# One hybrid decoder layer step with product-key experts: layout of the streamed one-hots, early expert products, gather pacing, buffers of the closing norms

## The chip, the cores and the metric

The kernel runs on one core of one Trainium2 chip, as one program on that core. The metric is device time in microseconds (us). TensorE (PE in the profile), its weight loads (PEld), VectorE (DVE), ScalarE (ACT), GpSimd (POOL) and SyncE (SP) each run a stream of instructions of their own; SP here does nothing but start DMA transfers.

## What is computed

One layer for 512 prompt tokens and 8 sample tokens (one new token each), width 1024, all in f32: a norm, one input projection into attention and retention heads, the two mixers, an output projection with residual; then a layer of single-neuron experts, and a final norm. The change lies in the expert layer and the final norm:

```
def _peer_block(xb, w_pq, sub_keys, peer_u, peer_v):
    q = (xb @ w_pq).reshape(blk, PEER_HEADS, 2, PEER_HALF)            # 8 heads, two halves of 128
    s = jnp.einsum('thcd,hcnd->thcn', q, sub_keys).astype(jnp.float32)  # 128 keys a half
    sv, si = lax.top_k(s, PEER_TOPK)                                  # 16 of 128, each half
    cand = (sv[:, :, 0, :, None] + sv[:, :, 1, None, :]).reshape(blk, PEER_HEADS, PEER_TOPK * PEER_TOPK)
    cidx = (si[:, :, 0, :, None] * PEER_N_KEYS + si[:, :, 1, None, :]).reshape(...)
    best, pos = lax.top_k(cand, PEER_TOPK)                            # 16 of the 256 pairs
    eid = jnp.take_along_axis(cidx, pos, -1)                          # expert i * 128 + j
    g = jax.nn.softmax(best, -1).astype(xb.dtype)
    u = peer_u[eid]
    a = jax.nn.gelu(jnp.einsum('thkd,td->thk', u, xb))
    return jnp.einsum('thk,thkd->td', g * a, peer_v[eid])
...
    h = hp + _mixer_output(attn_o, ret_o, rg, ret_gn_g[l], w_out[l])
    hp = _channel(h, norm2_g[l], w_pq[l], ...)                        # h + _peer(_rmsnorm(h))
y_prompt = _rmsnorm(hp, norm_f_g)
```

Each token thus uses 8 x 16 = 128 of 16,384 experts; peer_u and peer_v hold 1024 numbers for each expert.

## The kernel before

**Two ways to the same experts.** Prompt tokens 0 to 255 (lists 0 and 1) and the 8 samples (list S) are *gathered*; prompt tokens 256 to 511 (lists 2 and 3) are *dense*.

- A gather step handles one (head, k) of one list: GpSimd starts an indirect DMA that fetches for each of 128 tokens its expert's row (L898) into one of GBUFS = 8 buffers of the pool's tag "rows", and VectorE folds it in, either as a dot with the token (L914, peer_u, into a; its sum is read out by a second short instruction) or as a weighted sum into y (L928, peer_v). Lists 0 and 1 have 256 steps each, list S has 32 steps of 64 partitions (8 samples x 8 heads): 544 in all, each list's after the one before it.
- In the dense way every value of i (the first half of an expert's number) is a product row. `dense_a` multiplies the 128 experts i * 128 + j with the 256 tokens (L869: 8 products of 256 columns, weights ut, loaded by SP at L866 out of a table turned for it) and takes gelu of it (L873, tile ge). `dense_w` multiplies ge by the weight of each pair (L1048, tile big; zero for experts that a token didn't choose). `dense_y` sums over j (L1055: 4 products of 512 columns, against vt, loaded by SP at L1042) into four PSUM banks that stay open over all 128 rows.
- The weights in big come from one-hots: for a group of 8 tokens VectorE compares lists with a ramp (oj, L1026: 128 values of j x 8 tokens; oi, L1027: 64 values of i x 8 tokens), multiplies oi by the weight split into three bf16 parts (oi3, L1029), and TensorE multiplies, for each of the 8 tokens and the 3 parts, oj (as loaded weights) with oi3 (as the stream of 64 columns) (L1034): 24 products a group. ScalarE puts the result into big (L1036). There are 32 groups, once for i below 64 (`scatter(0, n)`, ahead of the first product row's `dense_w`) and once for i from 64 on (`scatter(1, n)`, between the first 64 rows).

**Stages.** Mixers and output projection to about 386 us. Then the product keys: for 8 heads, first of the gathered tokens and samples, then of the dense ones (`product_keys`, L148 projects with w_pq, which SP loads at L127; L805 and L810 give the scores, L814 copies them out, VectorE makes the top-16 lists). Among the dense tokens' heads `between(h)` emits the first EARLY = 96 gather steps; among the 32 groups of `scatter(0, n)` the next SOON = 48, and the first AHEAD = 20 of `dense_a`. The main loop then runs over i: `dense_a(i + 20)`, `dense_y(i - 1)`, `dense_w(i)`, and gather steps at (RATE - EARLY - SOON) / 128 = 3.28 a row. What is left of the steps follows, with the norm of each list (`finish`) at its end, and at the very end the norm of the dense tokens.

**What sets the order.** The source emits instructions in the order above; a scheduler then places them at build time, by a timeline of its own, on each engine, so that a step can stand later in an engine's stream than it is emitted. `tc.issue_after` keeps steps behind a given instruction, `in_order` (L1059) keeps TensorE's products of the main loop as written. SP's queue is followed in order. A tag's buffers go round: UTB = 4 for ut, VTB = 4 for vt, OHB = 2 for the one-hots, AHEAD + 2 for ge.

Of the kernel before, what the change touches and what calls it, by code (L numbers as in the profile page):

```python
# [19 lines left out]
D = 1024  # L20
# [11 lines left out]
GT = 256  # L32
NC = [(0, 256), (256, 520)]
DT = 512 - GT
GBUFS, UTB, VTB, OHB, AHEAD = 8, 4, 4, 2, 20
ORDER = "aayyyy"
FIRST = 6
SCB = 4
# [3 lines left out]
CHUNKS = [0, 64, 128]  # L42
ROWS = max(b - a for a, b in zip(CHUNKS, CHUNKS[1:]))
NG = DT // 8
EARLY, SOON, RATE = 96, 48, 564


@with_exitstack
def step_kernel(ctx, tc, x_prompt, x_sample, cache_k, cache_v, state_ret, norm1_g, w_in, ret_gn_g,
# [38 lines left out]
    def row_bcast(dst, src, n):  # L88
        nc.sync.dma_start(dst, bass.AP(tensor=src.tensor, offset=src.offset, ap=[[0, dst.shape[0]], [1, n]]))
# [786 lines left out]
    def run(g, n=1):  # L876
        for _ in range(n):
            if g is not None:
                next(g, None)
# [19 lines left out]
                                     in_offset=bass.IndirectOffsetOnAxis(ap=d["eid"][:p, h, k:k + 1], axis=0))  # L899
        return t  # L900

    def experts(d, rows):
        p, H = d["p"], d["H"]
        y = pe.tile([128, D], F32, name="y", tag="y")[:p]
        hn = pe.tile([128, D], F32, name="hq", tag="hq")[:p]
        for n, src in enumerate(rows):
            nc.sync.dma_start(hn[n * p // len(rows):(n + 1) * p // len(rows)], src)

        def dots(h):
            a = pe.tile([128, TOPK], F32, name="a", tag="a", bufs=3)[:p]  # L910
            for k in range(TOPK):
                yield
                u = gather(u_tab, d, h, k, "u")
                nc.vector.tensor_tensor_reduce(out=u[:p], in0=u[:p], in1=hn, scale=1.0, scalar=0.0,  # L914
                                               op0=OP.mult, op1=OP.add, accum_out=a[:, k:k + 1])
            w = pe.tile([128, TOPK], F32, name="gw", tag="gw", bufs=3)[:p]
            nc.scalar.activation(w, a, AF.Gelu_apprx_tanh)
            nc.vector.tensor_tensor(out=w, in0=w, in1=d["g"][:p, h, :], op=OP.mult)
            return w

        def sums(h, w):
            for k in range(TOPK):
# [12 lines left out]
        return y

    def finish(halves, p, rows, dst):
# [15 lines left out]
    yp2 = y_p.rearrange("a t d -> (a t) d")  # L953

    def gathered():
        y = yield from experts(lists[0], [hnr[:128, :]])
        finish((y[:, 0:512], y[:, 512:]), 128, slice(0, 128), yp2[0:128, :])
        y = yield from experts(lists[1], [hnr[128:GT, :]])
        finish((y[:, 0:512], y[:, 512:]), 128, slice(128, GT), yp2[128:GT, :])
        y64 = yield from experts(listS, [hnr[GT:, :]] * 8)  # L960
# [5 lines left out]
        finish((yS[:, 0:512], yS[:, 512:]), 8, slice(512, 520), y_s.rearrange("b t d -> (b t) d"))  # L966

    work = gathered()

    def between(h):  # L970
# [46 lines left out]
    def scatter(c, n):  # L1017

        t0 = n * 8
        r0, r1 = CHUNKS[c:c + 2]  # L1020
        ni = r1 - r0
        oj = dw.tile([128, 128, 8], BF16, name="oj", tag="oj", bufs=OHB)
# [13 lines left out]
        nc.scalar.activation(place(c, n), pg_.rearrange("p (t i) -> p t i", i=ni), AF.Copy)  # L1036

# [43 lines left out]
    def ahead():
        for i in range(AHEAD):
            g = dense_a(i)
            for _ in range(2):
                run(g)
                yield
# [88 lines left out]
```

## Time and profile before

| | |
|---|---|
| median of 3 runs | 1840.87 us (1839.99 to 1841.41) |
| the profiled execution | 1843.8 us, span of its records 1842.0 us |
| mean granted TensorE clock | 0.901 of full speed |
| busy: TensorE, VectorE, ScalarE, GpSimd | 1598.4, 1210.3, 366.4, 777.3 us |
| moved by DMA | 488.55 MB, mean 265 GB/s |

The span runs from the first to the last record of the profiled execution. Busy shares over the whole span mix stages with different limits, so the rows further down are by stage. An f32 product leaves two records on TensorE (1888 records of L869 in one bank and 160 in another are 128 rows x 8 products x 2). DMA share is the mean busy share of the core's 16 DMA engines.

### The profile page before, as it was taken

To read this page: it belongs to the slowest core of one execution; us is meant where nothing else is said; L and a number is where in the kernel's file an instruction comes from. 1 tells how busy PE (TensorE), PEld (TensorE's weight loads), DVE (VectorE), ACT (ScalarE), POOL (GpSimd) and SP (SyncE) were. 2 spreads that over 40 slices of the span, in tenths; PEclk is the share of its full clock that TensorE was granted. 3 is DMA by queue.
4 is the path that set the end of the run, shared out by engine and by line. 5 is a ranking of instruction groups with operands and counts; after the bars stand their busy time and mean duration, and the time that the engine had idled before them with its cause. 6 is when DMAs were issued, how large, how long until landed. Compare 5 with 4: busy or idle time off the path is not lost. (4 is left out here: it accounts for less than half of the span.)

```text
span 1842.0 us, 22181 instructions
## 1 busy us (share of the span) xinstructions
PE 1598.4 (87%) x7848; PEld 1206.4 (65%) x7848; DVE 1210.3 (66%) x2835; ACT 366.4 (20%) x727; POOL 777.3 (42%) x672
## 2 busy tenths in 40 slices
PE   5999998989877844789999999999999999999700
PEld 5888875968766734786777777776766666664300
DVE  5556654228999889999656555645555555557687
ACT  5554332532212111231101111111100000000001
POOL 2015521010472785645444332444445545546553
PEclk9999899989988975559999999999999999999955
DMA  5226554343797978668998888888889999999986
GB/s 180 68 70 184 168 164 128 109 155 121 242 367 237 327 270 322 216 189 304 357 331 292 324 311 284 315 322 313 286 298 390 362 361 360 361 348 380 387 255 151
DMA packets 182031, 488.55 MB, mean 265 GB/s; under 512 B 15848, under 2 KB 71704, under 8 KB 181920
## 3 DMA queue, kind: packets, MB, share of 16 engines
q0 software_dynamic: 82208, 295.80, 45.7%
q1 hardware_dynamic: 99712, 191.33, 29.6%
q8 instruction: 62, 1.02, 0.2%
q14 instruction: 49, 0.40, 0.1%
HBM read 477.21 MB, written 9.86 MB: 264 GB/s over the span
## 5 line engine op out<-in xcount | busy, mean ns | idle before, releaser
L898 POOL DMA_INDIRECT u<-in_peer_u,eidL x256 | 328.9, 1285 | 382.2 <-DVE y L928 119.8
L869 PE MATMUL pa<-hnD,ut 128*128 128x256 f32 x1888 | 451.7, 395 | 27.6 <-ACT ge L873 20.8
L1055 PE MATMUL y<-vt,ge 128*128 128x512 f32 x1024 | 460.2, 596 | 9.0 <-DMA vt<-in_peer_v 9.0
L898 POOL DMA_INDIRECT v<-in_peer_v,eidL x256 | 323.3, 1263 | 321.9 <-DVE y L928 148.2
L869 PEld LDWEIGHTS pa<-hnD,ut 128*128 128x128 f32 x1888 | 373.9, 200 | 114.8 <-issue 41.2
L928 DVE SCALAR_TENSOR_TENSOR y<-v,gw,y 128x1024 f32<-128x1024 f32 (+1 forms) x269 | 344.1, 1279 | 30.4 <-DMA v<-in_peer_v,eidL 25.0
L914 DVE CUSTOM_DVE_ANT_0 u<-u,hq 128x1024 f32<-128x1024 f32 (+1 forms) x272 | 324.5, 1221 | 20.9 <-DMA u<-in_peer_u,eidL 20.6
L1055 PEld LDWEIGHTS y<-vt,ge 128*128 128x128 f32 x1024 | 195.8, 191 | 211.4 <-issue 195.3
L1034 PEld LDWEIGHTS <-oj 128*128 128x128 bf16 x1536 | 186.6, 146 | 50.2 <-DVE oi L1029 32.2
L1048 DVE TENSOR_TENSOR ge<-ge,big 128x256 f32<-128x256 f32 x128 | 51.2, 422 | 194.5 <-ACT ge L873 181.3
L1034 PE MATMUL pg<-oi,oj 128*128 128x64 bf16 x1152 | 147.3, 301 | 19.3 <-DVE oi L1029 19.2
L873 ACT ACTIVATE ge<-pa 128x256 f32<-128x256 f32 x118 | 45.3, 384 | 555.9 <-PE pa L869 548.7
L1026 DVE TENSOR_TENSOR oj<-iota,lJ 128x1024 bf16<-128x1024 bf16 x64 | 44.1, 688 | 148.7 <-PE pg L1034 146.2
L117 PE MATMUL pa<-xT,wh 128*128 128x256 f32 (+1 forms) x448 | 135.6, 305 | 3.4 <-ACT xT L113 3.2
L118 PE MATMUL pa<-xT,wh 128*128 128x256 f32 (+1 forms) x448 | 132.5, 296 | 0.1
L119 PE MATMUL pa<-xT,wl 128*128 128x256 f32 (+1 forms) x448 | 130.6, 292 | 0.0
L1036 ACT ACTIVATE big<-pg 128x512 f32<-128x512 f32 x48 | 53.3, 1110 | 221.5 <-PE pg L1034 219.2
L117 PEld LDWEIGHTS pa<-xT,wh 128*128 128x128 f32 x448 | 85.5, 192 | 14.2 <-issue 8.1
L118 PEld LDWEIGHTS pa<-xT,wh 128*128 128x128 f32 x448 | 85.9, 192 | 6.2 <-issue 4.9
L119 PEld LDWEIGHTS pa<-xT,wl 128*128 128x128 f32 x448 | 85.9, 192 | 5.0 <-issue 4.1
L111 DVE TENSOR_TENSOR wl<-raw,wh 128x1024 fp32r<-128x1024 f32 x36 | 44.3, 1232 | 59.8 <-ACT wh L110 59.7
L148 PE MATMUL pa<-hnD,raw 128*128 128x256 f32 x256 | 62.5, 401 | 13.7 <-DMA raw<-in_w_pq 13.7
(464 smaller groups left out, 1725.8 us busy)
## 6 DMA issues: line engine op xcount, KB each, us to landing
ut<-in_u_turned SPq DMA_DIRECT2D x128, 512.0 KB
vt<-in_peer_v SPq DMA_DIRECT2D x128, 512.0 KB
raw<-in_w_pq SPq DMA_DIRECT2D x16, 1024.0 KB
raw<-in_w_in SPq DMA_DIRECT2D x28, 512.0 KB
kv<-in_cache_k_win POOLq DMA_DIRECT2D x24, 256.0 KB, 3.8
kv<-in_cache_v_win POOLq DMA_DIRECT2D x24, 256.0 KB, 4.5
raw<-in_w_out SPq DMA_DIRECT2D x4, 1024.0 KB
u<-in_peer_u,eidL POOLq DMA_INDIRECT x256, 7.7
```

The source lines that it names most:

```text
L117: nc.tensor.matmul(out, wh, xh, start=first, stop=False)
L118: nc.tensor.matmul(out, wh, xl, start=False, stop=False)
L119: nc.tensor.matmul(out, wl, xh, start=False, stop=last)
L148: nc.tensor.matmul(pa[:, :n], part[:, k, :], x[0][:, k, :], start=(k == 0), stop=(k == KB - 1))
L869: nc.tensor.matmul(pa, ut[:, k, :], hnD[:, k, :], start=(k == 0), stop=(k == KB - 1))
L898: nc.gpsimd.indirect_dma_start(out=t[:p], out_offset=None, in_=tab, in_offset=bass.IndirectOffsetOnAxis(ap=d["eid"][:p, h, k:k + 1], axis=0))
L914: nc.vector.tensor_tensor_reduce(out=u[:p], in0=u[:p], in1=hn, scale=1.0, scalar=0.0, op0=OP.mult, op1=OP.add, accum_out=a[:, k:k + 1])
L928: nc.vector.scalar_tensor_tensor(y, v[:p], w[:, k:k + 1], y, op0=OP.mult, op1=OP.add)
L1034: nc.tensor.matmul(pg_[:, t * ni:(t + 1) * ni], oj[:, :, t], oi3[:, z, :, t], start=(z == 0), stop=(z == 2))
L1036: nc.scalar.activation(place(c, n), pg_.rearrange("p (t i) -> p t i", i=ni), AF.Copy)
L1048: last_ = nc.vector.tensor_tensor(out=gs, in0=gs, in1=wt, op=OP.mult)
L1055: nc.tensor.matmul(yps[b][q], ge[:, b * 128:(b + 1) * 128], vt[:, q * 512:(q + 1) * 512], start=(i == 0), stop=(i == NKEY - 1))
```

## The change

Four things, and what follows from them for the order. Sizes, types and the number of gather steps stay.

1. **Streamed one-hots in runs of eight.** oi and oi3 held, for each i, 8 tokens side by side, so that the 64 columns streamed for one token lay 8 elements (16 bytes) apart. Now each holds, for each block of 8 values of i, 8 tokens x 8 values: a token's columns come as 8 runs of 8 neighbours. The comparison takes its list spread by eight, which a new ScalarE instruction per group makes (lx, L1056 of the changed kernel: 4 x 8 x 8 elements). oj, the loaded weights, is as before.
2. **First rows between the heads.** AHEAD0 = 14 of the rows that `ahead` emits now come in `between(h)`, through a bank of their own (paF), the other 5 among the one-hot groups.
3. **Pace.** EARLY 96 to 72, RATE 564 to 600 (in the source 3.75 gather steps a row instead of 3.28), AHEAD 20 to 19.
4. **Closing norms.** hx, gfb and fin leave the ring of the gathers for buffers of their own, hq has two; gfbG is loaded once, hx with the list's first sums; the output's store is emitted 12 steps into the next list.

```
-GBUFS, UTB, VTB, OHB, AHEAD = 8, 4, 4, 2, 20
+GBUFS, UTB, VTB, OHB, AHEAD = 8, 4, 4, 2, 19
-EARLY, SOON, RATE = 96, 48, 564
+EARLY, SOON, RATE = 72, 48, 600
+AHEAD0 = 14
...
-    def experts(d, rows):
+    def experts(d, rows, hr):
...
-        hn = pe.tile([128, D], F32, name="hq", tag="hq")[:p]
+        hn = pe.tile([128, D], F32, name="hq", tag="hq", bufs=2)[:p]
...
+        if hr.start == 0:
+            row_bcast(gfbG, norm_f_g, D)
...
         w = yield from dots(0)
+
+        x = pe.tile([128, D], F32, name="hx", tag="hx")
+        nc.sync.dma_start(x[:hr.stop - hr.start], hs[hr, :])
...
-        x = gp.tile([128, D], F32, name="hx", tag="rows")
-        nc.sync.dma_start(x[:p], hs[rows, :])
...
-        gfb = gp.tile([128, D], F32, name="gfb", tag="rows")
-        row_bcast(gfb, norm_f_g, D)
-        o = gp.tile([128, D], F32, name="fin", tag="rows")
+        o = pe.tile([128, D], F32, name="fin", tag="fin")
...
-        nc.vector.scalar_tensor_tensor(o[:p], x[:p], r[:p], gfb[:p], op0=OP.mult, op1=OP.mult)
-        nc.sync.dma_start(dst, o[:p])
+        nc.vector.scalar_tensor_tensor(o[:p], x[:p], r[:p], gfbG[:p], op0=OP.mult, op1=OP.mult)
+        return lambda: nc.sync.dma_start(dst, o[:p])
...
+        y, x = yield from delayed(experts(lists[1], [hnr[128:GT, :]], slice(128, GT)), 12, store)
...
+    def ahead():
+        for i in range(AHEAD):
+            g = dense_a(i)
+            for _ in range(2):
+                run(g)
+                yield
+    first = ahead()
+    banks["a"] = lambda: ps_tile("tr", "paF")

     def between(h):
         run(work, EARLY * (h + 1) // PH - EARLY * h // PH)
+        run(first, 2 * (AHEAD0 * (h + 1) // PH - AHEAD0 * h // PH))
...
-        oi = dw.tile([128, ni, 8], BF16, name="oi", tag="oi", bufs=OHB)
-        oi3 = dw.tile([128, 3, ni, 8], BF16, name="oi3", tag="oi3", bufs=OHB)
+        oi = dw.tile([128, ne, 64], BF16, name="oi", tag="oi", bufs=OHB)
+        oi3 = dw.tile([128, 3, ne, 64], BF16, name="oi3", tag="oi3", bufs=OHB)
         ts = slice(t0, t0 + 8)
+        nc.scalar.activation(lx.rearrange("p q (t e) -> p q t e", e=8),
+                             l5[:, 1:, ts][:, :, :, None].to_broadcast([128, 4, 8, 8]), AF.Copy)
...
-        nc.vector.tensor_tensor(out=oi, in0=iota128[:, r0:r1], in1=lI[:, None, ts].to_broadcast([128, ni, 8]),
+        nc.vector.tensor_tensor(out=oi.rearrange("p a (t e) -> p a t e", e=8),
+                                in0=iotaE[:, r0 // 8:r1 // 8, None].to_broadcast([128, ne, 8, 8]),
+                                in1=lx[:, 0:1].rearrange("p q (t e) -> p q t e", e=8).to_broadcast([128, ne, 8, 8]),
                                 op=OP.is_equal)
-        marks[c] = nc.vector.tensor_tensor(out=oi3, in0=oi[:, None].to_broadcast([128, 3, ni, 8]),
-                                           in1=lg3[:, :, ts][:, :, None, :].to_broadcast([128, 3, ni, 8]), op=OP.mult)
+        marks[c] = nc.vector.tensor_tensor(out=oi3, in0=oi[:, None].to_broadcast([128, 3, ne, 64]),
+                                           in1=lx[:, 1:, None].to_broadcast([128, 3, ne, 64]), op=OP.mult)
...
-                nc.tensor.matmul(pg_[:, t * ni:(t + 1) * ni], oj[:, :, t], oi3[:, z, :, t], start=(z == 0),
+                es = slice(t * 8, t * 8 + 8)
+                nc.tensor.matmul(pg_[:, t * ni:(t + 1) * ni], oj[:, :, t], oi3[:, z, :, es], start=(z == 0),
                                  stop=(z == 2))
...
-    first = ahead()
+    rest = 2 * (AHEAD - AHEAD0)
     for n in range(NG):
         scatter(0, n)
-        run(first, 2 * AHEAD * (n + 1) // NG - 2 * AHEAD * n // NG)
+        run(first, rest * (n + 1) // NG - rest * n // NG)
```

**What moves on each engine.** Counted in the order of instructions: on VectorE 92 gather steps stood ahead of the first one-hot, now 71; ahead of the first `dense_w` 138, now 118; ahead of the last one 448, now 435. On TensorE 24 rows of `dense_a` stood ahead of the first one-hot product, now 23. On ScalarE lx of group n + 3 stands ahead of the evacuation into big of group n + 1. Line numbers of the changed kernel are those of before plus 1 (L148 is L149) up to plus 36 (L1042 is L1078).

TensorE, among the product-key heads of the gathered tokens (pss and psco are the scores, L805 and L810 before), before:

```order
L148 MATMUL pa<-hn,raw 128x264 x8
L805 MATMUL pss<-qT,keysT 128x8
L810 MATMUL psco<-keysT,qT 128x128
L148 MATMUL pa<-hn,raw 128x264 x8
L805 MATMUL pss<-qT,keysT 128x8
L810 MATMUL psco<-keysT,qT 128x128 x3
L148 MATMUL pa<-hn,raw 128x264 x8
```

and of the change:

```order
L811 MATMUL psco<-keysT,qT 128x128
L870 MATMUL paF<-hnD,ut 128x256 x8
L149 MATMUL pa<-hn,raw 128x264 x2
L806 MATMUL pss<-qT,keysT 128x8
L811 MATMUL psco<-keysT,qT 128x128 x3
L149 MATMUL pa<-hn,raw 128x264 x14
L870 MATMUL paF<-hnD,ut 128x256 x3
L806 MATMUL pss<-qT,keysT 128x8
L811 MATMUL psco<-keysT,qT 128x128
```

The 8 products of the first early row and 3 of the second now stand in front of the scores of heads 2 and 3, and later ones in front of later scores; five whole rows come ahead of the last scores.

SyncE's queue, from the stores of the norm's output (hnr) on, before:

```order
L778 DMA hnr<-xg 128x1024 x2
L907 DMA hq<-hnr 128x1024
L127 DMA raw<-in_w_pq 128x8x256 x13
L866 DMA ut<-in_u_turned 128x1024 x27
L1042 DMA vt<-in_peer_v 128x1024 x4
```

and of the change:

```order
L779 DMA hnr<-xg 128x1024 x2
L908 DMA hq<-hnr 128x1024
L867 DMA ut<-in_u_turned 128x1024 x4
L128 DMA raw<-in_w_pq 128x8x256
L908 DMA hq<-hnr 128x1024
L128 DMA raw<-in_w_pq 128x8x256
L867 DMA ut<-in_u_turned 128x1024
L128 DMA raw<-in_w_pq 128x8x256 x11
L867 DMA ut<-in_u_turned 128x1024 x21
L1078 DMA vt<-in_peer_v 128x1024 x4
```

Five loads of ut stand ahead of w_pq loads that they followed, four of them ahead of the one of head 3.

VectorE, where the second list ends and the samples begin, before:

```order
L928 SCALAR_TENSOR_TENSOR y<-v,gw,y 128x1024 x32
L943 TENSOR_TENSOR hx<-y,hx 128x512 x2
L99 TENSOR_SCALAR rv__11850<-ssqf 128x1
L101 RECIPROCAL rr__11851<-rt__11852 128x1
L102 TENSOR_TENSOR rt__11852<-rr__11851 128x1
L103 SCALAR_TENSOR_TENSOR rt__11852<-rt__11852,rv__11850 128x1
L104 SCALAR_TENSOR_TENSOR rr__11851<-rt__11852,rr__11851 128x1
L950 SCALAR_TENSOR_TENSOR fin<-hx,rr__11851,gfb 128x1024
L914 ISA u,a<-u,hq 64x1024
```

and of the change:

```order
L931 SCALAR_TENSOR_TENSOR y<-v,gw,y 128x1024 x31
L917 ISA u,a<-u,hq 64x1024
L917 ISA a 64x1
L947 TENSOR_TENSOR hx<-y,hx 128x512 x2
L917 ISA u,a<-u,hq 64x1024
L917 ISA a 64x1
```

The samples' first dot now stands ahead of the norm's additions, and the norm's other instructions between later dots.

## Rows read from the trace of the kernel before

**Rows 1.** Stages: from:to, us; busy (instructions) by engine; clock; DMA share, GB/s.

```profile
474.00:708.40 234.40, 156.62 (x652) 130.98 (x650) 219.18 (x847) 32.55 (x79) 155.57 (x100) 0.83 0.84 301
708.40:831.70 123.30, 97.70 (x776) 93.16 (x777) 117.72 (x180) 35.76 (x34) 65.63 (x47) 0.50 0.69 226
831.70:1361.00 529.30, 529.30 (x2231) 378.22 (x2229) 313.73 (x457) 64.49 (x105) 222.45 (x191) 0.97 0.86 317
1361.00:1661.50 300.50, 300.50 (x1048) 199.54 (x1047) 167.19 (x249) 17.56 (x48) 149.57 (x119) 1.00 0.95 351
1661.50:1747.00 85.50, 76.47 (x175) 33.43 (x173) 60.73 (x67) 0.30 (x2) 48.93 (x46) 0.96 1.01 386
1747.00:1773.40 26.40, 0.38 (x1) 0.00 (x0) 21.20 (x17) 0.00 (x0) 15.96 (x15) 0.60 0.99 347
1773.40:1842.00 68.60, 3.58 (x4) 0.37 (x4) 52.11 (x79) 11.03 (x21) 27.16 (x28) 0.50 0.67 156
```

**Rows 2.** TensorE's groups, 831.7 to 1361 us: records; busy us, mean ns; idle before.

```profile
L869 PE MATMUL pa<-hnD,ut 128*128 128x256 f32 x964 | 229.6, 393 | 0.0
L1055 PE MATMUL y<-vt,ge 128*128 128x512 f32 x504 | 228.1, 596 | 0.0
L1034 PE MATMUL pg<-oi,oj 128*128 128x64 bf16 x763 | 97.9, 301 | 0.0
```

**Rows 3.** Timeline pieces: start, us, engine, operation, records (idle before).

```profile
17.05 0.92 PEld L383 LDWEIGHTS ptS<-ident,x1s 8*128 8x128 f32 x8 [0.33 <-issue]
...
716.40 5.88 PEld L1034 LDWEIGHTS <-oj 128*128 128x128 bf16 x49 [11.89 <-DVE oi L1029]
...
999.89 2.34 PEld L1034 LDWEIGHTS <-oj 128*128 128x128 bf16 x19
...
1002.33 3.63 PE L869 MATMUL pa<-hnD,ut 128*128 128x256 f32 x16
1005.80 3.60 PE L1055 MATMUL y<-vt,ge 128*128 128x512 f32 x8
1009.23 2.97 PE L869 MATMUL pa<-hnD,ut 128*128 128x256 f32 x13
```

**Rows 4.** One line's weight loads: ns least/median/most, first and last start.

```profile
L1034 PEld LDWEIGHTS <-oj x1536: 141/146/174, 716.4 to 1359.3; 128*128 128x128 bf16 x192
...
L869 PEld LDWEIGHTS pa<-hnD,ut x1888: 186/190/338, 551.3 to 1660.4; 128*128 128x128 f32 x189
```

**Rows 5.** One line's instructions on VectorE and ScalarE, columns as in rows 4.

```profile
L914 DVE CUSTOM_DVE_ANT_0 u<-u,hq x272: 1193/1218/1293, 490.4 to 1797.7; 128x1024 f32<-128x1024 f32 x128, 64x1024 f32<-64x1024 f32 x8
L914 DVE DVE_READ_ACCUMULATOR2_ANT a<- x272: 70/79/84, 491.5 to 1798.8; 128x1 f32 x128, 64x1 f32 x8
...
L928 DVE SCALAR_TENSOR_TENSOR y<-v,gw,y x269: 1243/1279/1286, 555.5 to 1819.9; 128x1024 f32<-128x1024 f32 x127, 64x1024 f32<-64x1024 f32 x8
...
L1048 DVE TENSOR_TENSOR ge<-ge,big x128: 409/424/469, 831.7 to 1661.5; 128x256 f32<-128x256 f32 x128
...
L873 ACT ACTIVATE ge<-pa x118: 360/384/406, 578.9 to 1661.1; 128x256 f32<-128x256 f32 x118
```

**Rows 6.** VectorE's busy time up to 831.7 us: L914, then L928.

```profile
0.00:831.70 831.70, 96.61 (x160) 0.86 0.59 195
...
0.00:831.70 831.70, 72.47 (x57) 0.86 0.59 195
```

**Rows 7.** Waits, 388 to 474 us: who for whom, us in all, times, longest.

```profile
DVE valL L254 <- ACT sc L814: 17.7, 4, 6.6
```

**Rows 8.** Timeline, VectorE, the end of the second list.

```profile
1772.08 1.28 DVE L928 SCALAR_TENSOR_TENSOR y<-v,gw,y 128x1024 f32<-128x1024 f32 x1 [3.70 <-DMA v<-in_peer_v,eidL]
1773.40 1.29 DVE L943 TENSOR_TENSOR hx<-y,hx 128x512 f32<-128x512 f32 x2
...
1779.41 1.21 DVE L914 CUSTOM_DVE_ANT_0 u<-u,hq 64x1024 f32<-64x1024 f32 x1
```

More of the change, by code (lines that the diff above doesn't have):

```diff
@@ L934, in experts, with finish @@
             w = w2
-        return y
-    def finish(halves, p, rows, dst):
-        x = gp.tile([128, D], F32, name="hx", tag="rows")
-        nc.sync.dma_start(x[:p], hs[rows, :])
+        return y, x
+    def finish(halves, p, x, dst):
         for q, y in enumerate(halves):
@@ L949, in finish, with delayed @@
         r = rstd_of(ssq[:p], D, 1e-6, p)
-        nc.vector.scalar_tensor_tensor(o[:p], x[:p], r[:p], gfb[:p], op0=OP.mult, op1=OP.mult)
-        nc.sync.dma_start(dst, o[:p])
+        nc.vector.scalar_tensor_tensor(o[:p], x[:p], r[:p], gfbG[:p], op0=OP.mult, op1=OP.mult)
+        return lambda: nc.sync.dma_start(dst, o[:p])
+    def delayed(g, n, f):
+        while True:
+            try:
+                next(g)
+            except StopIteration as e:
+                return e.value
+            n -= 1
+            if n == 0:
+                f()
+            yield
     yp2 = y_p.rearrange("a t d -> (a t) d")
+    gfbG = pe.tile([128, D], F32, name="gfbG", tag="gfbG")
     def gathered():
[L956 to L960, printed above, removed]
+        y, x = yield from experts(lists[0], [hnr[:128, :]], slice(0, 128))
+        store = finish((y[:, 0:512], y[:, 512:]), 128, x, yp2[0:128, :])
+        y, x = yield from delayed(experts(lists[1], [hnr[128:GT, :]], slice(128, GT)), 12, store)
+        store = finish((y[:, 0:512], y[:, 512:]), 128, x, yp2[128:GT, :])
+        y64, x = yield from delayed(experts(listS, [hnr[GT:, :]] * 8, slice(512, 520)), 12, store)
         yS = gp.tile([128, D], F32, name="yS", tag="rows")[:8]
@@ L965, in gathered @@
             nc.scalar.activation(yS[:, q * 512:(q + 1) * 512], ph[:8], AF.Copy)
-        finish((yS[:, 0:512], yS[:, 512:]), 8, slice(512, 520), y_s.rearrange("b t d -> (b t) d"))
+        finish((yS[:, 0:512], yS[:, 512:]), 8, x, y_s.rearrange("b t d -> (b t) d"))()
     work = gathered()
+    def ahead():
[3 more added lines that the diff above has]
+                run(g)
+                yield
+    first = ahead()
+    banks["a"] = lambda: ps_tile("tr", "paF")
     def between(h):
         run(work, EARLY * (h + 1) // PH - EARLY * h // PH)
+        run(first, 2 * (AHEAD0 * (h + 1) // PH - AHEAD0 * h // PH))
     product_keys(lists, listS, hn, between)
@@ L988, in step_kernel @@
     nc.vector.tensor_copy(iota128, iota128f[:, :, None].to_broadcast([128, 128, 8]))
-    lI = dn.tile([128, DT], BF16, name="lI")
-    lJ = dn.tile([128, DT], BF16, name="lJ")
+    iotaE = dn.tile([128, 16, 8], BF16, name="iotaE")
+    nc.vector.tensor_copy(iotaE, iota128f.rearrange("p (a b) -> p a b", b=8))
+    l5 = dn.tile([128, 5, DT], BF16, name="l5")
+    lJ, lI, lg3 = l5[:, 0], l5[:, 1], l5[:, 2:]
     lg = dw.tile([128, DT], F32, name="lgt", tag="lgt")
-    lg3 = dn.tile([128, 3, DT], BF16, name="lg3")
     for b in (2, 3):
@@ L1021, in scatter @@
         ni = r1 - r0
+        ne = ni // 8
+        lx = dw.tile([128, 4, 64], BF16, name="lx", tag="lx", bufs=OHB)
         oj = dw.tile([128, 128, 8], BF16, name="oj", tag="oj", bufs=OHB)
-        oi = dw.tile([128, ni, 8], BF16, name="oi", tag="oi", bufs=OHB)
-        oi3 = dw.tile([128, 3, ni, 8], BF16, name="oi3", tag="oi3", bufs=OHB)
+        oi = dw.tile([128, ne, 64], BF16, name="oi", tag="oi", bufs=OHB)
+        oi3 = dw.tile([128, 3, ne, 64], BF16, name="oi3", tag="oi3", bufs=OHB)
         ts = slice(t0, t0 + 8)
+        nc.scalar.activation(lx.rearrange("p q (t e) -> p q t e", e=8),
+                             l5[:, 1:, ts][:, :, :, None].to_broadcast([128, 4, 8, 8]), AF.Copy)
         nc.vector.tensor_tensor(out=oj, in0=iota128, in1=lJ[:, None, ts].to_broadcast([128, 128, 8]), op=OP.is_equal)
-        nc.vector.tensor_tensor(out=oi, in0=iota128[:, r0:r1], in1=lI[:, None, ts].to_broadcast([128, ni, 8]),
+        nc.vector.tensor_tensor(out=oi.rearrange("p a (t e) -> p a t e", e=8),
+                                in0=iotaE[:, r0 // 8:r1 // 8, None].to_broadcast([128, ne, 8, 8]),
+                                in1=lx[:, 0:1].rearrange("p q (t e) -> p q t e", e=8).to_broadcast([128, ne, 8, 8]),
                                 op=OP.is_equal)
-        marks[c] = nc.vector.tensor_tensor(out=oi3, in0=oi[:, None].to_broadcast([128, 3, ni, 8]),
-                                           in1=lg3[:, :, ts][:, :, None, :].to_broadcast([128, 3, ni, 8]), op=OP.mult)
+        marks[c] = nc.vector.tensor_tensor(out=oi3, in0=oi[:, None].to_broadcast([128, 3, ne, 64]),
+                                           in1=lx[:, 1:, None].to_broadcast([128, 3, ne, 64]), op=OP.mult)
         pg_ = (pgs if c else pgs + [yps[0][0], yps[1][0]])[n % (2 if c else 4)]
@@ L1079, in step_kernel @@
     ring += [yps[0][1], yps[1][1]]
[L1081 to L1086, printed above, removed]
-    first = ahead()
+    rest = 2 * (AHEAD - AHEAD0)
     for n in range(NG):
         scatter(0, n)
-        run(first, 2 * AHEAD * (n + 1) // NG - 2 * AHEAD * n // NG)
+        run(first, rest * (n + 1) // NG - rest * n // NG)
         with tc.issue_after(marks[0].ins):
```

## The prediction

> **What bounds the kernel now.** I read a table of busy time by stage first, then groups of instructions, then single pieces of the timeline. A gather step fetches 128 expert rows (0.524 MB) and folds them in with one VectorE instruction, a dot (L914) or a sum (L928). A product row is one value of i: 8 products of 256 columns (L869) and 4 of 512 (L1055); an f32 product counts as two instructions.
>
> From 474 to 708.4 us VectorE is busy for 219.18 of 234.40 us with the top-16 lists and the first gather steps, and TensorE waits for it. [...] The first product row is multiplied by its weights at 831.7 us, the last at 1661.5 us [rows 5].
>
> Between those two TensorE is the bound. Up to 1361 us it started 964 instructions of L869, 504 of L1055 and 763 of the one-hot products, L1034 [rows 2]. In the timeline 16 of L869 take 3.47 us until the next group starts (0.216 us each), 8 of L1055 take 3.43 us (0.429), and weight loads of L1034 come one per 0.120 to 0.123 us: 49 in 5.88 us, 19 in 2.34 us [rows 3]. So 964 x 0.216 + 504 x 0.429 + 763 x 0.122 = 517 of the 529.3 us. Gathers follow VectorE's order meanwhile: 80 dots (160 records of L914) and 58 sums (57 of L928, and the first one of another line) are done at 831.7 us, 138 steps in all [rows 6]; 448 stand ahead of the last product row's multiplication. After that DMA is the bound: its share is 1.01 and 0.99, and TensorE needs 85.5 us for rows that are 20 x 3.43 = 69 us of work [rows 1]. The last step of the second list ends at 1773.4 us [rows 8]; 32 steps for the samples and the closing norms take the last 68.6 us.
>
> **Edit 1: 24 fewer gather steps among the product-key heads, and five product rows there instead.** In VectorE's order 71 steps stand ahead of the first one-hot instead of 92, and 118 instead of 138 ahead of the first product row. 21 steps at 1.22 + 0.07 us (L914) or 1.28 us (L928) [rows 5] are 27 us, off a stage in which VectorE idles for 15 us only. The five rows cost TensorE 5 x 3.46 = 17 us. VectorE has a backlog from the fourth head on, which hides most of that; before, it waits for scores four times, 17.7 us in all [rows 7], and 8 + 3 products (4.8 us) now stand ahead of scores of heads 2 and 3. On SP's queue four ut loads (2.1 MB) pass the w_pq load of head 3; at the 301 GB/s of the next stage they take 7 us [rows 1], which is the bound on what that load may come late, and I take none of it, as its buffer comes free two projections ahead. So 27 - 5 = **22 us earlier** (bounds 0 and 27): first product row at 809.7 us. The other early rows fill idle time of TensorE in either kernel: 24 rows stand ahead of the one-hots before, 23 now.
>
> **Edit 2: the streamed one-hot in runs of eight.** Before, the 64 streamed columns lay 16 bytes apart; now they come in runs of eight neighbours. The weights stay 16 bytes apart. No row shows the new form. The load of these weights has a record of 146 ns, that of f32 weights 190 ns [rows 4], and f32 loads ahead of 8-column products follow each other at 0.106 us (8 in 0.92 us, the last one of 0.18 us counted off, [rows 3]). A load that is shorter by 0.044 us should then allow about 0.062 us. So I hold the stream, not the load, for what takes 0.122 us, 1.9 ns a column, also because this pace is the same at a granted clock of 0.50 and near 1. The bounds for the new pace are 0.062 and 0.122; I take 0.066, just over the load's estimate. In the main loop 768 products save 768 x 0.056 = **43 us** of TensorE. In the first 32 groups they save nothing: 24 x 0.122 = 2.9 us of TensorE a group lie under VectorE's 117.72 / 32 = 3.7. [...] No row here shows a stream of the new kind.
>
> The new copy that spreads the lists by eight (lx) is a ScalarE instruction of 256 elements, as ge is (0.38 us, [rows 5]). ScalarE is busy for 36 of 123 us and 64 of 529 us where it lands [rows 1], and in its order lx(n+3) stands ahead of big(n+1), so that VectorE has it early. Without that cover it would cost 32 x 0.4 = 13 us ahead of the first row. VectorE's three one-hot instructions keep their sizes and have neighbours innermost as before, so I cost them alike.
>
> **Edit 3: pace and AHEAD.** The steps per row rise in the source, but in VectorE's order 435 steps stand ahead of the last product row instead of 448: most of the 20 that were put off are not caught up. With AHEAD at 19 one more L869 row and one more L1055 row come before that point, 6.9 us. So the last row is multiplied at 809.7 + 829.8 + 6.9 - 43 = 1603 us. From there to the last step of the second list it was 111.9 us, in which 386 x 85.5 + 347 x 26.4 = 42.2 MB moved [rows 1], 377 GB/s. 13 steps more and one vt load less are 6.3 MB, 17 us. By TensorE's and VectorE's order that step ends at **1732 us**.
>
> **DMA over the whole stretch.** From the first product row to that step 167.8 + 105.5 + 33.0 + 9.2 = 315.4 MB moved in 941.7 us, 335 GB/s [rows 1]. Now 20 more gathers and one more ut load have to fit: 326.4 MB. In 922 us that would be 354 GB/s, more than the 351 of the stage from 1361 us, where DMA's share was 0.95 and TensorE still kept its pace. I take 351: 930 us, so that step ends at **1739.6** instead of 1773.4 us.
>
> **Edit 4: own buffers for the closing norms.** Before, VectorE does the second list's norm alone, from 1773.40 us to the samples' first dot at 1779.41 [rows 8]. Now its instructions lie between the samples' dots. Of the 6.0 us the adds (1.29), the last product (as long as a sum, 1.28) and five short ones stay, some 3.4: **2.6 us** saved of the last 68.6 (bounds 0 and 6).
>
> **Sum.** 1739.6 + 68.6 - 2.6 = 1805.6 us of span. The profiled execution took 1843.8 us, 1.8 over its span, and the median of the runs is 2.9 below that: 1805.6 + 1.8 - 2.9 = **1804 us**.
>
> **Rivals.**
> - Weight load: these weights hold the pace at the f32 load's 0.106 us. Then 768 x 0.016 = 12 us are saved instead of 43, the step ends at 1732 + 31 = 1763 us, the total is 1828. Against it: the shorter record of the load. [...] Chance 0.12.
> - No change in the stream: 0.122 us stays, since the sequencer or the weights set it. 1732 + 43 = 1775 us, total 1840, nothing to measure. For it: the pace is the same at both clocks. Chance 0.15.
> - DMA keeps its mean of 335 GB/s, since gathers still come in bursts behind product rows: 974 us, 1784 us, total **1849**, slower. It decides from about 338 GB/s down. For it: 317 GB/s at a share of 0.86 up to 1361 us. Against it: the idle share there was TensorE's pace, which rises. Chance 0.10.
> - Key stage and loop both do better (27 us, and DMA no limit): 1727 us, total 1792 or a little less. Chance 0.08.
>
> **How the numbers follow.** The sum's own case has 0.55, and 1790 to 1820 with its bounds. The range runs from 1784 to 1842: it takes in the first two rivals and leaves out the slower one and the far end of the best. A measurement of this kernel tells 0.2%, 3.7 us, from no change. Faster: 0.55 + 0.12 + 0.08 and a fifth of the second rival, 0.78. Same: the rest of that rival, 0.12. Slower: 0.10.
>
> **What would show it.** Weight loads of the one-hot products one per 0.066 us in the main loop (stream), 0.106 (load) or 0.122 (neither). The first product row's multiplication near 810 us, the last near 1603. DMA's share at 0.95 or more and some 350 GB/s from the first product row on. The samples' first dot within 2 us of the last list step. I am wrong if L869 waits for ut, or L1055 for vt, before 1600 us, or if VectorE waits for lx or for scores by more than 10 us beyond what it did.

## The result and the profile after

The changed kernel takes 1770.62 us (median of 4 runs, 1760.83 to 1773.88) against 1841.14 (median of 4): a ratio of 0.9606, 95% interval 0.9567 to 0.9646, 3.9% faster. The forecast was 1804 us, in a range from 1784 to 1842: right in direction, 33 us too slow, and the measured time lies below the whole range. The profiled execution took 1771.55 us, with a span of 1769.8.

By stage, in us, with the forecast's own terms (first product row 809.7, its loop 829.8 + 6.9 - 43, last list step 1739.6, 68.6 - 2.6 behind it):

| | before | forecast | after |
|---|---|---|---|
| first one-hot at | 708.4 | 686.4 | 683.0 |
| from there to the first product row | 123.3 | 123.3 | 117.1 |
| first to last product row | 829.8 | 793.7 | 782.6 |
| to the second list's last step | 111.9 | 136.2 | 123.4 |
| to the end | 68.6 | 66.0 | 63.7 |
| span | 1842.0 | 1805.6 | 1769.8 |

Every stage came out shorter than forecast, by 3.4, 6.2, 11.1, 12.8 and 2.3 us. From the second row of the table on, the stages are called the one-hot stage, the loop, the tail and the end below. The busy time by stage, after (columns as in [rows 1]):

```profile
683.00:800.10 117.10, 53.27 (x768) 49.37 (x768) 116.56 (x182) 49.01 (x68) 80.28 (x46) 0.50 0.71 227
800.10:1582.70 782.60, 782.15 (x3306) 530.48 (x3307) 491.16 (x711) 94.15 (x184) 391.16 (x318) 1.00 0.95 355
1582.70:1706.10 123.40, 71.63 (x167) 31.35 (x165) 97.13 (x110) 0.45 (x3) 85.00 (x76) 0.80 1.01 384
1706.10:1769.80 63.70, 3.58 (x4) 0.37 (x4) 50.97 (x79) 10.81 (x21) 26.14 (x25) 0.50 0.61 155
```
TensorE is still the bound of the loop (busy for 782.15 of 782.60 us), now at a granted clock of 1.00 and with DMA at 0.95 and 355 GB/s. In the tail DMA is full (1.01, 384 GB/s). The timeline where [rows 3] and [rows 8] have theirs: weight loads of one-hot products in the one-hot stage and in the loop, and the place where the samples begin:

```profile
794.85 1.53 PEld L1070 LDWEIGHTS <-oj 128*128 128x128 bf16 x24 [2.63 <-DVE oi L1064]
...
998.81 1.48 PEld L1070 LDWEIGHTS <-oj 128*128 128x128 bf16 x23 [0.29 <-issue]
...
1704.81 1.28 DVE L931 SCALAR_TENSOR_TENSOR y<-v,gw,y 128x1024 f32<-128x1024 f32 x1 [2.33 <-DMA v<-in_peer_v,eidL]
1706.01 1.21 DVE L917 CUSTOM_DVE_ANT_0 u<-u,hq 64x1024 f32<-64x1024 f32 x1
...
1707.16 1.28 DVE L947 TENSOR_TENSOR hx<-y,hx 128x512 f32<-128x512 f32 x2
```

Loads of one-hots follow each other in 0.061 us ((1.48 - 0.14) / 22), half of what they took; the forecast was 0.066. The record of one load is longer than before all the same (least, median, most, ns; it was 146 in [rows 4]):

```profile
L1070 PEld LDWEIGHTS <-oj x1536: 140/171/178, 688.0 to 1275.4; 128*128 128x128 bf16 x192
```

The samples' first dot follows at once on the last sum, the norm's additions behind it. One line's instructions, as in [rows 5]: the new copy on ScalarE, and the product rows' multiplication:

```profile
L1057 ACT ACTIVATE lx<-l x64: 399/416/437, 685.9 to 1216.2; 128x256 bf16<-128x256 bf16 x64
...
L1084 DVE TENSOR_TENSOR ge<-ge,big x128: 408/424/493, 800.1 to 1582.7; 128x256 f32<-128x256 f32 x128
```

The copy takes 0.42 us, and VectorE waited for it 1.1 us in all.

### The profile page after: what moved, and what is told of

The parts are those of the page before. It is cut to its first block, busy times and chain, and to the rows that moved or that the text cites. A ratio compares the mean times of both kernels' runs of the same rounds, so it can differ in the third digit from the quotient of the medians.

```text
span 1769.8 us, 22243 instructions
## 1 busy us (share of the span) xinstructions
PE 1485.1 (84%) x7848; PEld 1101.4 (62%) x7848; DVE 1209.6 (68%) x2836; ACT 397.7 (22%) x796; POOL 816.8 (46%) x672
## 4 chain that ended last, share of the span: by engine, by line
PE 48%; DVE 21%; issue 15%; DMA 8%; POOL 6%; ACT 1%; SPq 0%; DVEq 0%; POOLq 0%; another core or an unknown queue 0%; ACTq 0%
PE y L1091 14%; PE pa L870 13%; DVE u L917 5%; DVE y L931 3%; PE pa L118 3%; PE pa L120 3%; PE pa L119 3%; POOL v L899 3%; DMA u<-in_peer_u,eidL 3%; PE pg L1070 3%; DMA v<-in_peer_v,eidL 2%; POOL u L899 2%; PE pa L149 2%; DVE oi L1064 2%; DMA pq<-sq_d 1%
## 5 line engine op out<-in xcount | busy, mean ns | idle before, releaser
L899 POOL DMA_INDIRECT u<-in_peer_u,eidL x256 | 348.5, 1361 | 329.9 <-DVE y L931 97.8
L899 POOL DMA_INDIRECT v<-in_peer_v,eidL x256 | 342.7, 1339 | 270.3 <-DVE y L931 119.5
L870 PE MATMUL pa<-hnD,ut 128*128 128x256 f32 x1792 | 409.1, 382 | 5.0 <-ACT ge L874 4.4
L870 PEld LDWEIGHTS pa<-hnD,ut 128*128 128x128 f32 x1792 | 340.0, 191 | 82.7 <-issue 35.7
L1070 PEld LDWEIGHTS <-oj 128*128 128x128 bf16 x1536 | 101.4, 168 | 81.5 <-DVE oi L1064 62.2
L1070 PE MATMUL pg<-oi,oj 128*128 128x64 bf16 x1152 | 77.8, 232 | 32.5 <-DVE oi L1064 32.5
L1059 DVE TENSOR_TENSOR oj<-iota,l 128x1024 bf16<-128x1024 bf16 x64 | 43.7, 686 | 87.3 <-PE pg L1070 84.2
L979 PE MATMUL pa<-y,selT 64*8 64x512 f32 x4 | 3.6, 1048 | 96.9 <-DVE y L931 96.9
```

The lines of the kernel that those rows point to most:

```text
L870: nc.tensor.matmul(pa, ut[:, k, :], hnD[:, k, :], start=(k == 0), stop=(k == KB - 1))
L899: nc.gpsimd.indirect_dma_start(out=t[:p], out_offset=None, in_=tab, in_offset=bass.IndirectOffsetOnAxis(ap=d["eid"][:p, h, k:k + 1], axis=0))
```

## The experiments

Ratios and differences are to the kernel before as timed beside each experiment (medians from 1841.61 to 1844.67 us), unless said otherwise. "Stream" is edit 2 of the prediction, "norms" edit 4, "pacing" edits 1 and 3.

**The stream alone.** Of the diff only the hunks on l5, iotaE, lx, oi, oi3 and the product's `es`.

> The kernel before with edit 2 alone (streamed one-hots in runs of eight, lx). Theory A: nearly all of the gain is the stream's. In the changed kernel's trace 47 weight loads of L1070 take 2.93 us (0.061 us each, 0.122 before), 47 us over the main loop's 768 products; the one-hot stage and the rest of the loop, which were 6 and 7 us shorter than the forecast, go with it. Then about 60 us faster, 1781 us, with some 117 us from the first one-hot to the first product row instead of 123, and the first one-hot still at 708 us. Theory B: only the pace itself, 47 us, 1794 us, and the other 13 us come from the early rows and the pacing. Theory C, that of the forecast (DMA holds 351 GB/s at most): 315 MB in 899 us, some 40 us faster, 1800 us.

1777.81 us, a ratio of 0.9654 (0.9622 to 0.9687), 63.8 us faster: theory A, and C falls. By stage:

```profile
709.60:826.50 116.90, 53.16 (x781) 49.83 (x782) 116.36 (x180) 47.89 (x69) 83.24 (x47) 0.53 0.72 234
826.50:1599.10 772.60, 772.60 (x3273) 524.53 (x3271) 481.88 (x708) 94.11 (x182) 386.70 (x312) 1.00 0.95 355
1599.10:1709.00 109.90, 78.34 (x175) 33.89 (x173) 80.50 (x81) 0.22 (x1) 62.06 (x59) 0.86 1.01 378
1709.00:1777.10 68.10, 3.58 (x4) 0.36 (x4) 52.10 (x79) 11.03 (x21) 26.85 (x28) 0.50 0.66 158
```
The loop is 57.2 us shorter (772.6 against 829.8). 768 x 0.061 = 47 of them are the pace. The other 10 come from a clock that no longer falls. In the kernel before, TensorE never paused in the loop (busy for 829.8 of 829.8 us), and yet its clock fell in seven places, each time behind a group of one-hot products; one of them in windows of 2 us:

```profile
896.00:898.00 2.00, 2.00 (x19) 2.00 (x18) 0.01 (x1) 0.00 (x0) 1.70 (x2) 1.00 1.00 410
898.00:900.00 2.00, 2.00 (x11) 1.82 (x10) 0.99 (x2) 0.99 (x1) 0.07 (x1) 0.69 1.01 410
900.00:902.00 2.00, 2.00 (x6) 1.55 (x6) 1.97 (x3) 0.12 (x1) 0.00 (x0) 0.50 1.05 422
902.00:904.00 2.00, 2.00 (x11) 1.76 (x10) 1.51 (x2) 0.00 (x0) 1.50 (x1) 0.96 0.83 332
```

and its timeline there:

```profile
892.46 3.60 PE L1055 MATMUL y<-vt,ge 128*128 128x512 f32 x8
895.89 3.08 PE L1034 MATMUL pg<-oi,oj 128*128 128x64 bf16 x24
898.79 5.32 PE L869 MATMUL pa<-hnD,ut 128*128 128x256 f32 x16
```

The granted clock (third column from the end) goes from 1.00 to 0.50 when 24 slow products (3.08 us) have just run, and the next product row takes 5.32 us where others take 3.62. Over the loop 54 instructions of L869 take 0.34 to 0.50 us until the next one starts instead of 0.216, 11.4 us more in all. With the stream changed none takes more than 0.30, and at such a place TensorE's timeline reads

```profile
1003.38 3.60 PE L1064 MATMUL y<-vt,ge 128*128 128x512 f32 x8
1006.81 1.59 PE L1043 MATMUL pg<-oi,oj 128*128 128x64 bf16 x24
1008.24 3.70 PE L869 MATMUL pa<-hnD,ut 128*128 128x256 f32 x16
```
The one-hot stage is 6.4 us shorter, which the forecast had at nothing. VectorE's group of oj in it (busy us, mean ns, idle before and what ended it), before, and under it with the stream alone:

```profile
L1026 DVE TENSOR_TENSOR oj<-iota,lJ 128x1024 bf16<-128x1024 bf16 x34 | 23.3, 686 | 4.8 <-PE y L1034 2.5 <-PE pg L1034 2.3
```

```profile
L1032 DVE TENSOR_TENSOR oj<-iota,l 128x1024 bf16<-128x1024 bf16 x34 | 23.2, 683 | 0.0
```
Before, VectorE waited 4.8 us for a one-hot buffer (there are two) that TensorE's products still read; now it doesn't. These waits are 4.8 of the 6.4 us; the rest was not traced. That 2.9 us of products a group lie under 3.7 us of VectorE was true on average, not for each group.

**The pacing alone.** EARLY 72, RATE 600, AHEAD 19, `first` begun in `between`.

> The kernel before with edits 1 and 3 alone (early rows between the heads, EARLY 72, RATE 600, AHEAD 19). In VectorE's order 71 steps stand ahead of the first one-hot and 433 ahead of the last product row. Theory A: the first one-hot comes 25 us earlier, the loop is 6.9 us longer for the row more, the tail some 14 us longer for 15 steps more: about 5 us faster, 1836 us. Theory B: also the 6 us of the one-hot stage and the 7 of the loop: about 18 us faster, 1823 us. Theory C, that of the forecast: 22 us gained, 6.9 and 20 given back, 5 us slower, 1846 us.

1847.38 us, 1.0036 (1.0018 to 1.0054): 5.8 us slower, theory C, the forecast's own arithmetic.

```profile
806.20:1643.60 837.40, 836.88 (x3306) 582.69 (x3307) 489.43 (x707) 82.39 (x154) 397.31 (x316) 0.98 0.91 332
1643.60:1773.40 129.80, 71.62 (x167) 31.35 (x165) 99.54 (x113) 0.44 (x3) 87.87 (x75) 0.78 1.00 381
1773.40:1841.80 68.40, 3.58 (x4) 0.36 (x4) 52.09 (x79) 11.03 (x21) 26.94 (x28) 0.50 0.67 158
```
The first one-hot comes at 682.7 us, 25.7 earlier; the loop is 7.6 longer (6.9 forecast), the tail 17.9 longer for 15 more steps. The profiled execution (1843.55 us) is the fastest of this kernel's ten: in it gain and cost cancel to 0.2 us, so it shows where they arise, and not the 5.8 us. What was moved out of VectorE's way ahead of the first row was paid for by DMA behind the last one.

**The norms alone.** hq with two buffers, hx, gfbG and fin of their own, stores put off.

> The kernel before with edit 4 alone (own buffers for the closing norms, stores put off). The forecast: 2.6 us faster. The changed kernel's trace has 63.8 us from the last step of the second list to the end instead of 68.6, so theory A: 4.8 us faster, 1836 us, all of it behind 1773 us. Rival: the ring of the gathers was also held up at the first list's norm, so that more is won, some 10 us, and part of it shows before 1773 us.

1826.01 us, 0.9909 (0.9879 to 0.9938): 15.6 us faster, six times the forecast's 2.6 and also above theory A. The rival is right that part of it shows before the list's end, though the ring, its reason, is not shown by that:

```profile
831.30:1659.20 827.90, 827.90 (x3277) 576.29 (x3275) 482.06 (x707) 81.88 (x153) 381.69 (x311) 0.98 0.90 330
1659.20:1766.20 107.00, 75.03 (x175) 32.87 (x173) 80.57 (x82) 0.21 (x1) 66.69 (x62) 0.87 1.00 378
1766.20:1827.40 61.20, 3.58 (x4) 0.36 (x4) 50.81 (x79) 10.81 (x21) 26.37 (x25) 0.50 0.67 159
```
The tail is 4.9 us shorter, the end 7.4, the loop 1.9. In that last stage all 6.0 us between the last sum and the samples' first dot are gone, not 2.6, and the norm's instructions between the dots cost little: from the samples' first dot to their last sum it takes 41.5 us (1766.1 to 1807.6) instead of 40.5 (1779.4 to 1819.9).

**The second hq buffer alone.**
```
-        hn = pe.tile([128, D], F32, name="hq", tag="hq")[:p]
+        hn = pe.tile([128, D], F32, name="hq", tag="hq", bufs=2)[:p]
```


> The kernel before with one line changed: two buffers for the gathered tokens (hq), so that the samples' tokens can be loaded before the second list's last dot. In the kernel before, the queue of SyncE holds four vt loads behind that load, and TensorE waits 9.0 us for vt at 1731 us. Theory A: that wait goes and with it the part of edit 4 that shows before the second list's end (4.9 us): 1836 us. Theory B: the tail goes by bytes, the wait is off the path: 1841 us, and all of edit 4 is in the ring and the place of the norms.

1837.39 us, 0.9974 (0.9956 to 0.9991): 6.1 us faster, theory A. Two waits of the kernel before (who for whom, us in all, times, longest), in the tail:

```profile
PE y L1055 <- DMA vt<-in_peer_v: 9.0, 1, 9.0
SPq L907 <- DVE a L914: 8.6, 1, 8.6
```

SyncE's queue in the tail (start, us, transfers), before, and under it with the second buffer:

```profile
1643.81 65.62 SPq L1042 DMA_DIRECT2D vt<-in_peer_v  x17
1718.08 2.65 SPq L907 DMA_DIRECT2D hq<-hnr  x8
1723.13 2.95 SPq L1042 DMA_DIRECT2D vt<-in_peer_v  x4
```

```profile
1640.83 79.35 SPq L1042 DMA_DIRECT2D vt<-in_peer_v  x21
```
Eight loads of the samples' tokens waited for the second list's last dot, and four vt loads behind them; TensorE waited 9.0 us for vt. Now the 21 vt loads go in one piece, and TensorE has no such wait. The tail is 108.3 us instead of 111.9 in the trace, so that 3.6 of the 6.1 us are seen there; the first product row was also 3.2 us earlier, which the edit does not explain: up to the first one-hot the instructions of TensorE, VectorE and ScalarE stand in the same order in both. Part of the gain of edit 4 is thus not in the closing norms at all.

**The changed kernel with the old stream.** The stream's hunks undone.

> The changed kernel with edit 2 undone (one-hots as before, 16 bytes apart; the rest of the change kept). Theory A: 60 us slower than the changed kernel, 1831 us; weight loads of the one-hot products one per 0.122 us again. Theory B: 47 us slower, 1818 us. If the parts add up, this run and the one with edit 2 alone have the same difference to their neighbours.

1833.77 us, 0.9963 (0.9943 to 0.9982) of the kernel before, and 63.2 us slower than the changed one: as much as the stream gains alone, so the parts add up (-63.8 + 5.8 - 15.6 = -73.6, measured -70.5). Its loop has the falls of the clock again, seven of them, 11.9 us.

**Streamed columns 8 bytes apart.** On the kernel before; a single run.
```
+        oi = dw.tile([128, 2, ni, 4], BF16, name="oi", tag="oi", bufs=OHB)
+        oi3 = dw.tile([128, 3, 2, ni * 4], BF16, name="oi3", tag="oi3", bufs=OHB)
...
+                                 oi3[:, z, t // 4].rearrange("p (a t) -> p a t", t=4)[:, :, t % 4], ...)
```


> The kernel before with the 64 streamed columns 8 bytes apart instead of 16 (groups of four tokens instead of eight; VectorE's oi and oi3 in two instructions each; the weights as before). Only TensorE's pace is read. [...] Theory B: any column that is not the neighbour of the one before costs 1.9 ns: 0.122 us as before.

The timeline of weight loads in the loop:

```profile
1010.74 1.48 PEld L1040 LDWEIGHTS <-oj 128*128 128x128 bf16 x23 [0.29 <-issue]
```
The pace is 0.061 us ((1.48 - 0.14) / 22; 1785.01 us in all): theory B falls. The columns need not be neighbours; half the distance was enough to bring the stream down to 0.061 us, the pace that the weights set in the changed kernel. Whether such a stream would be faster still with packed weights, this run can't tell.

**The loaded one-hots laid out by token too.** On the changed kernel; VectorE reads the list of j out of lx.
```
-        oj = dw.tile([128, 128, 8], BF16, name="oj", tag="oj", bufs=OHB)
+        oj = dw.tile([128, 8, 128], BF16, name="oj", tag="oj", bufs=OHB)
...
-                nc.tensor.matmul(pg_[:, t * ni:(t + 1) * ni], oj[:, :, t], oi3[:, z, :, es], ...)
+                nc.tensor.matmul(pg_[:, t * ni:(t + 1) * ni], oj[:, t], oi3[:, z, :, es], ...)
```


> The changed kernel, with the loaded one-hots (oj) laid out by token too, so that a token's 128 weights are neighbours; lx then holds the list of j as well (5 x 64 elements). Theory A: 0.061 us is what this load of 128 columns needs wherever they lie: pace and time as in the changed kernel, 1771 us within 4. Theory B: the 16 bytes between the weights cost as much as those between streamed columns did: pace near 0.03 us, 768 x 0.03 = 23 us less in the loop, 1748 us. Theory C: VectorE's oj becomes slower (its list operand is read in runs of eight): more than 0.69 us each, 64 x that difference later.

1746.44 us, 0.9482 (0.9463 to 0.9502), 24.2 us faster than the changed kernel: theory B. The timeline of weight loads in the loop:

```profile
912.76 0.74 PEld L1073 LDWEIGHTS <-oj 128*128 128x128 bf16 x23 [0.33 <-issue]
```

The pace is (0.74 - 0.10) / 22 = 0.029 us. One line's instructions show VectorE's oj at 0.68 us, as before:

```profile
L1059 DVE TENSOR_TENSOR oj<-iotaE,lx x64: 672/683/709, 680.7 to 1219.4; 128x1024 bf16<-128x1024 bf16 x64
```

By stage:

```profile
796.30:1555.60 759.30, 758.83 (x3306) 505.51 (x3307) 491.24 (x712) 95.27 (x184) 388.29 (x318) 1.00 0.97 366
1555.60:1678.60 123.00, 71.54 (x167) 31.35 (x165) 97.02 (x110) 0.43 (x2) 81.19 (x76) 0.81 1.01 386
```

The loop is 23.3 us shorter (768 x 0.032 = 25), and DMA moves 366 GB/s in it.

**The same on the kernel before, the stream left as it was.** A single run.

> The kernel before with the loaded one-hots laid out by token (weights are neighbours) and the streamed ones as before, 16 bytes apart. Only TensorE's pace and granted clock are read. Theory A: load and stream run side by side, so the slower of the two sets the pace: 0.122 us as before, with the clock falling after groups in the loop as before. Theory B: their costs add: 0.122 - 0.032 = 0.09 us.

The timeline of weight loads in the loop:

```profile
915.99 2.65 PEld L1042 LDWEIGHTS <-oj 128*128 128x128 bf16 x23 [0.33 <-issue]
```
0.115 to 0.116 us ((2.65 - 0.10) / 22), and 1843.41 us: theory A, though 0.006 us under the 0.122 of the kernel before. Load and stream run side by side, and the slower sets the pace: a stream 16 bytes apart 0.12, weights 16 bytes apart 0.06, both packed 0.03. The clock falls nine times in this loop.

**Stream and norms without the pacing.** AHEAD 19, EARLY 96, RATE 564, no early rows.

> The kernel before with edits 2 and 4 and AHEAD 19 (with 20 the buffers don't fit), without the early rows and with EARLY 96 and RATE 564 as before. In VectorE's order 95 steps stand ahead of the first one-hot, 138 ahead of the first product row, 452 ahead of the last. If the parts add up, 64 us from the stream and 15 us from the norms, less 3 for the row that AHEAD 19 adds: 1765 us, some 5 us faster than the changed kernel, since the early rows and the pacing cost 6 us by themselves. Rival: with the faster stream the pacing pays (more steps fit under less TensorE time), and this kernel is 5 us or more slower than the changed one.

1765.03 us, 0.9575 (0.9559 to 0.9591): as the sum says, 5.6 us faster than the changed kernel. The intervals of the two ratios overlap (0.9567 to 0.9646 there), so this difference by itself is not clear of noise; that the pacing pays 5 us with the faster stream, the rival, is not borne out.

**The changed kernel without the early rows.** The hunks on `first` and `between` undone, the constants kept.

> The changed kernel without the early rows between the heads (edit 1's second half undone); EARLY 72, RATE 600 and AHEAD 19 kept, so that 71 gather steps stand ahead of the first one-hot and 435 ahead of the last product row as in the changed kernel, and 23 rows ahead of the first one-hot product, but none ahead of the last scores. Theory A: TensorE is idle enough behind the heads that the early rows win nothing: 1771 us within 4, first product row near 800 us. Theory B: they fill time that is missing later, and the first product row comes up to 17 us later: 1788 us. Theory C: they hold up scores and w_pq loads, and without them the lists are done earlier: some 5 us faster, 1766 us.

1760.71 us, 0.9547 (0.9533 to 0.9562), 9.9 us faster than the changed kernel: beyond theory C; but one of the changed kernel's four runs took 1760.83 us too. The first row is 6.5 us earlier (793.6 us), the end 2.7 shorter. Such a shift in single executions says little: this kernel and the last one below have the same order of instructions on TensorE, VectorE and ScalarE up to the first one-hot, and start it at 676.6 and at 682.4 us.

**The early rows from the fifth head on.**
```
-        run(first, 2 * (AHEAD0 * (h + 1) // PH - AHEAD0 * h // PH))
+        run(first, 2 * (AHEAD0 * max(h - 3, 0) // 4 - AHEAD0 * max(h - 4, 0) // 4))
```


> The changed kernel with its 14 early rows emitted only from the fifth head on; in TensorE's order they then all stand behind the last scores, and their ut loads behind all w_pq loads, in the bank of their own (paF) as before. Theory A: what the early rows cost (10 us against the kernel without them) is their place ahead of scores and w_pq loads: 1761 us, last scores copied out near 545 us, first one-hot near 677. Theory B: it is the bank of their own, in which row waits for gelu after gelu: 1771 us, with the scores early and the first one-hot products late.

1769.94 us, 0.9609 (0.9579 to 0.9638), no better than the changed kernel, though the last scores came 7 us earlier (their products start at 545.7 us, in the changed kernel at 552.5). So their place ahead of the scores does not explain the 10 us; theory A falls. B isn't shown either: TensorE did wait 28.1 us for that bank (between 540 and 690 us), but the one-hot stage is no longer for it (117.2 us, without early rows 117.0). The first row came at 797.6 us, only 4.0 later than without early rows, and the end took 66.0 us instead of 61.0, with one wait of VectorE there (the waits: who for whom, us, times, longest) whose releaser is none of the engines:

```profile
DVE rt__11888 L104 <- remote: 4.2, 1, 4.2
```

**Both layouts, norms, no early rows**, with EARLY 96 and RATE 564, and then with EARLY 72 and RATE 600.

> Edits 2 and 4 with AHEAD 19, EARLY 96 and RATE 564, no early rows, and the loaded one-hots laid out by token as well. If the parts add up: the run with edits 2 and 4 (1765 us) less the 24 us that the loaded one-hots' layout took off the changed kernel: 1741 us, and some 30 us, 1.7%, faster than the changed kernel. Rival: DMA, at a share of 0.97 and 366 GB/s in the loop of that run, has no more to give, and this one ends at 1746 us or later too.

1742.95 us, 0.9445 (0.9416 to 0.9474): 5.5% faster than the kernel before, 27.7 us less than the changed kernel. That is nearer to the sum's 1741 than to the rival's 1746, but the interval takes in both.

> The kernel of the last but one comparison (edits 2 and 4, AHEAD 19, loaded one-hots by token, no early rows) with EARLY 72 and RATE 600, as the changed kernel has them. Without early rows these were 4 us faster than EARLY 96 and RATE 564 (1760.7 against 1765.0 us, in two calls). If that holds with the faster loads: 1738 us, 32 us faster than the changed kernel. Rival: a step ahead of the first row costs VectorE as much as it costs DMA behind the last one, and the 4 us were noise between calls: 1743 us.

1746.15 us, 0.948 (0.9455 to 0.9506): no gain from the pacing, the rival holds; nor is it told apart from the kernel with early rows and both layouts (1746.44).

## Why the forecast missed

What failed is the size of two terms and a bound laid over the sum, all on the same side; even the forecast's best rival, 1792 us, is 21 us too slow.

1. **Edit 2, "768 x 0.056 = 43 us".** That the stream set the pace was right, and so was 0.061 to 0.066 us; the layout of the weights set the next floor, as the bound of 0.062 said. That this bound came out was in part luck: it took a load record shorter by 0.044 us for a pace shorter by as much, but at 0.061 us that record is 171 ns, and packed weights have 100 ns at 0.029 us, where the same rule gives 0.087 and 0.016. The term measured 63.8 us: 47 are the pace, and two effects were missing, the falls of the clock (11 us) and the first 32 groups ("they save nothing": 6.4 us, 4.8 of them VectorE's waits). The first could have been read from [rows 1], a clock of 0.97 in a stage in which TensorE was busy throughout, and from the forecast's own sum for that stage, 517 of 529.3 us: all seven falls begin in it.
2. **Edit 4, "2.6 us".** It measured 15.6 (11 to 22). Costing only the interval between two lists left out what else the shared buffers held up: the single hq buffer with vt loads behind it on SyncE's queue (6.1 us, interval 2 to 8), and the gaps into which the norm fits. The forecast put TensorE's slow last rows (85.5 us for 69 us of work) down to DMA; 9.0 us of that is the wait for vt behind hq. No run takes the other 9.5 us apart; the trace of the norms alone has 7.4 us in the end and 1.9 in the loop.
3. **DMA, "351 GB/s at most".** It added 7.6 us to the tail (12.8 too long there; the norms are most of the rest), and they did not come: 355 GB/s in the loop with the stream alone, 366 with both layouts, and 359 in the changed kernel over the whole stretch from the first product row to the second list's last step. The 351 was read in a stage that TensorE bounded, and [rows 1] has 386 in the stage after it. The kernel's mean before (335) was what TensorE's pace asked for over most of that stretch, which the slower rival's own counter-argument said. That rival is refuted.
4. **Edits 1 and 3** were sized well: -22, +6.9 and +17 forecast, -25.7, +7.6 and +17.9 in the trace, 5.8 us slower by themselves in the median. But the early rows, which the forecast gave only 5 us of cost, took 10 us in one comparison and nothing in another (with both layouts), and the cause stays open.

The rivals of the weight load (0.106 us) and of no change in the stream (0.122) fall at the first timeline: the loads of the bf16 one-hots come one per 61 ns in it and, with the weights packed, one per 29.

## What to carry to other kernels

Where many short products run, look at the distance of neighbouring elements in both operands: load and stream overlapped here, and the slower set the pace (0.12 us with both 16 bytes apart, 0.06 with the stream packed, 0.03 with both packed), so pack both. Where an engine is busy throughout and its clock in the table is still below 1.00, look for the instructions ahead of each fall: making those faster gave back 11 us here beyond the 47 of their own. A step taken from ahead of the bound and put behind it is worth nothing if the stretch behind is full of DMA (the pacing alone, at a DMA share of 1.00 in the tail, was 5.8 us slower); and a buffer's price is found in the queue of whoever waits for it, not only where its own work stands (a second hq buffer gave 6.1 us).

## What the runs showed that I had not expected

- TensorE's clock falls without any pause of the engine: in each of six kernels whose one-hot products took 0.115 to 0.122 us (24 in 2.8 to 3.1 us), six to nine times in a loop, for 10 to 15 us in all (its mean over the loop is 0.98 in the four of them read by stage); in none of nine kernels with 0.061 or 0.029 us (1.00 in the seven read by stage). That slow products of this kind are the cause is shown only by this going together.
- With weights packed, the record of their load falls from 171 to 100 ns (medians), and the pace in the loop to 0.029 us, at a granted clock of 1.00. In the one-hot stage of the same kernel, at a granted clock of 0.50, it is 0.05 us (24 in 1.30 us):

```profile
780.93 1.30 PEld L1073 LDWEIGHTS <-oj 128*128 128x128 bf16 x24 [2.87 <-DVE oi L1067]
```

So the pace with both operands packed changed with the clock, while 0.122 us [rows 3] and 0.061 us (24 in 1.53 us at 0.50, 23 in 1.48 at 1.00) were the same at either level.
